# Moving the split of the gated output and the order of scores and values in a two-layer hybrid encoder step

## The chip, the cores and the metric

The kernel runs on one core of a Trainium2 chip. The metric is the device time of one execution in microseconds. Engines are named as the profile names them: PE (TensorE, with PEld for its weight loads), ACT (ScalarE), DVE (VectorE), POOL (GpSimd) and SP (SyncE). SP issues nearly all loads of weights; POOL issues the loads of the caches, the small stores and the DMAs that finish a transposition.

## What is computed

The reference is one inference step of a two-layer trunk over 384 rows: 256 rows of a new stream ("prompt") and 8 x 16 rows of running streams ("sample"), each of width 2048, all in float32.

```python
# layer 0
p = rmsnorm(h) @ w_in0          # q, k, v, gate of 8 forgetting heads, the same of 8 stick-breaking heads, 8 forget logits
fo = softmax(q k^T * scale + F_q - F_k, causal) v              # per head; sample rows also see 128 cached rows
so = exp(log_sigmoid(z) + sum of log_sigmoid(-z) after it) v   # z = q k^T * scale, strictly causal
h = h + concat(fo * silu(fz), so * silu(sz)) @ w_out0
# layer 1
u, v, z = split(rmsnorm(h) @ w_in1)
h = h + (u * (W_s layernorm(v) + b) * silu(z)) @ w_out1
y = rmsnorm(h)
```

The keys, the values and the log forget gates of layer 0 and the normalised v of the sample rows are outputs too.

## The kernel before

**Products.** The 384 rows are three blocks of 128 (`NT`). A product with a weight matrix runs over columns in blocks of 512 and over the depth in units of 128 rows. Each float32 operand is split into a high part in a reduced float32 format (`F32R`) and the rest: ACT copies the high part (L84 for weights), DVE subtracts (L86). Each unit then takes three matmuls per row block (L101 to L103): high by high, high by rest, rest by high. `dense_nat` runs one column block: for each pair of units it calls `wunit` twice (load on SP, split) and `products` once. It accumulates into three PSUM banks of the pool "d", which has four. Its argument `between` maps a depth index to a function that is called ahead of that pair; the instructions traced in it are ordered, each on its own engine, behind the last weight split that was traced. Weight buffers: five "raw", four "whi", four "wlo".

**Layer 0.** It runs in four groups of four heads (`quad`), groups 0 and 1 forgetting heads, 2 and 3 stick-breaking heads. A group projects k and q (`turned`), v (`values`), runs its four heads (`head`) and projects the gate. A projection is evicted from PSUM by ACT (`evict`, L400). k and q are then turned (`turn`): one DVE block transposition into a slot and 16 DMAs issued on POOL (L127). The gate becomes silu on ACT and DVE (L459 to L464), is multiplied with the heads' outputs `mixn` (L465), and is turned into `mT`, which shares its one buffer with the turned q. `mT` is split into a high and a rest part (`mixhi`, `mixlo`; L473, L474) for the output product `w_out0`. Behind that come the projections of the next group.

**A head.** POOL builds the forget mask `fb` (L486 to L492); DVE transposes the cached keys (L499); PE computes scores of prompt and sample rows into two banks of the pool "a", which has four (L503 to L508). DVE and ACT make probabilities `pr` (L520 to L526, or L530 to L541). PE transposes them (L545), ACT copies them to `PT` (L547), PE multiplies with the values (L553 to L561), DVE puts the result into `mixn` (L564 to L567). The cached keys and values (`kcache`, `vcache`) and `fb` have two buffers each.

**Output product of layer 0.** Its first two column blocks are done in two parts: the depth units 0 to 11 for both (`early`), then 12 to 15 (`rest`). The second block accumulates in three banks of the pool "a".

**Order.** The program is traced in the order of the code; a planner with costs of its own then sets the order of instructions on each engine, by that order as priority and by what it takes to be ready. Only `tc.issue_after` (used by `then` at the start and by `between`) fixes an order by hand. Engines run their queues in order.

**Start.** x is loaded in pieces on SP and, for the sample rows of the first two pieces, on ACT's queue (L154). The load of the norm's gains `graw` is the first on ACT's queue (L163). PE transposes the gains (L167) and x (L211); ACT and DVE make the high part and the rest (L214, L215); the first product is that of k of group 0, columns 1024 to 1535.

## Time and profile before

| | before |
|---|---|
| median of 3 runs | 1888.44 us (1886.86 to 1889.18) |
| profiled execution | 1889.66 us |
| its span | 1887.9 us |
| PE busy | 1816.4 us, 96% of the span |
| DVE busy | 922.8 us, 49% |
| ACT busy | 726.2 us, 38% |
| POOL busy | 401.2 us, 21% |
| mean granted clock of PE | 0.981 |
| layer 0's heads, first scores to last values | 150.5 to 705.0 us |

The profile is that of one execution. A row of a group or of the timeline names the source line, the engine, the operation, the tile that is written and the tiles that are read, and the shape; "xN" is the number of instructions in it. In brackets stands the time that the engine was idle before, and what released it. A releaser is inferred from the semaphore events: where an instruction waits for several, it is the one that came last. A matmul of plain float32 operands shows as two records, one of reduced operands as one; records of a stream overlap, so the pace is read from their starts.

### The profile page before, as it was taken

To read this page: it belongs to the slowest core of one execution; us is meant where nothing else is said; L and a number is where in the kernel's file an instruction comes from. 1 tells how busy PE (TensorE), PEld (TensorE's weight loads), DVE (VectorE), ACT (ScalarE), POOL (GpSimd) and SP (SyncE) were. 2 spreads that over 40 slices of the span, in tenths; PEclk is the share of its full clock that TensorE was granted. 3 is DMA by queue.
4 is the path that set the end of the run, shared out by engine and by line. 5 is a ranking of instruction groups with operands and counts; after the bars stand their busy time and mean duration, and the time that the engine had idled before them with its cause. 6 is when DMAs were issued, how large, how long until landed. Compare 5 with 4: busy or idle time off the path is not lost. (4 is left out here: it accounts for less than half of the span.)

```text
span 1887.9 us, 24617 instructions
## 1 busy us (share of the span) xinstructions
PE 1816.4 (96%) x8655; PEld 1497.2 (79%) x8655; DVE 922.8 (49%) x1541; ACT 726.2 (38%) x1294; POOL 401.2 (21%) x640
## 2 busy tenths in 40 slices
PE   8999599989959989999999999999999999999998
PEld 6987487878848868888888888888888888888887
DVE  4445434634643564553443535535644563554466
ACT  4435233534623544443333333232333333333334
POOL 1543633332152102220020013202102210220020
PEclk9999799999979989999999999999999999999999
DMA  5866556655545537764444345445535544454543
GB/s 177 212 172 160 140 163 176 171 146 165 148 123 156 151 90 226 206 189 128 129 138 125 123 141 155 140 137 146 153 124 153 143 140 150 139 141 134 178 143 120
DMA packets 160140, 285.63 MB, mean 151 GB/s; under 512 B 23768, under 2 KB 39056, under 8 KB 160016
## 3 DMA queue, kind: packets, MB, share of 16 engines
q1 hardware_dynamic: 127424, 225.37, 40.2%
q0 software_dynamic: 25072, 54.10, 11.3%
q10 hardware_dynamic: 7520, 4.60, 0.8%
q8 instruction: 68, 1.11, 0.3%
q14 instruction: 56, 0.46, 0.1%
HBM read 253.50 MB, written 14.74 MB: 142 GB/s over the span
## 5 line engine op out<-in xcount | busy, mean ns | idle before, releaser
L102 PE MATMUL d<-wlo,slot 128*128 128x512 f32 x2352 | 923.7, 394 | 0.1
L103 PE MATMUL d<-whi,slot 128*128 128x512 f32 x2352 | 916.7, 391 | 0.0
L86 DVE TENSOR_TENSOR wlo<-raw,whi 128x512 fp32r<-128x512 f32 x784 | 540.5, 698 | 769.0 <-ACT whi L84 768.3
L101 PE MATMUL d<-whi,slot 128*128 128x512 f32 x2352 | 826.1, 393 | 43.0 <-ACT slot L400 41.8
L84 ACT ACTIVATE whi<-raw 128x512 fp32r<-128x512 f32 x784 | 494.2, 631 | 909.0 <-PE d L103 843.4
L101 PEld LDWEIGHTS d<-whi,slot 128*128 128x128 f32 x2352 | 443.8, 189 | 138.9 <-ACT slot L400 42.7
L102 PEld LDWEIGHTS d<-wlo,slot 128*128 128x128 f32 x2352 | 444.2, 189 | 94.0 <-issue 1.2
L103 PEld LDWEIGHTS d<-whi,slot 128*128 128x128 f32 x2352 | 443.9, 189 | 94.1 <-issue 2.5
L127 POOL DMA_DIRECT2D gTt<-trn x128 | 78.2, 618 | 446.4 <-issue 262.8
L127 POOL DMA_DIRECT2D qT<-slot x64 | 39.1, 619 | 83.1 <-DVE slot L124 81.7
L127 POOL DMA_DIRECT2D mT<-slot x64 | 39.1, 618 | 49.8 <-issue 40.3
L127 POOL DMA_DIRECT2D kT<-slot x64 | 39.3, 621 | 8.1 <-DVE slot L124 3.2
L706 POOL DMA_DIRECT2D wr<-in_w_sp_dram x64 | 35.0, 554 | 27.7 <-DVE wT L710 25.9
L699 DVE TENSOR_TENSOR slot<-d,slot 128x512 f32<-128x512 f32 x48 | 32.0, 687 | 12.4 <-PE d L103 12.4
L656 POOL DMA_DIRECT2D slot<-in_sgu_ln_g_dram x8 | 4.5, 566 | 134.0 <-PE d L103 134.0
L428 POOL DMA_DIRECT2D vcache<-in_cache_sb_v_dram x8 | 7.2, 896 | 120.5 <-PE a L557 102.2
L426 POOL DMA_DIRECT2D kcache<-in_cache_sb_k_dram x32 | 25.1, 791 | 18.9 <-DVE KT L499 12.3
L545 PE MATMUL a<-ident,pr 128*128 128x128 f32 x96 | 17.8, 284 | 11.5 <-ACT pr L541 10.0
L380 PE MATMUL d<-wlo,slot 128*128 128x264 f32 (+1 forms) x96 | 27.2, 286 | 0.6 <-DVE wlo L91 0.6
L379 PE MATMUL d<-whi,slot 128*128 128x264 f32 (+1 forms) x96 | 26.7, 287 | 0.5 <-ACT slot L400 0.5
L381 PE MATMUL d<-whi,slot 128*128 128x264 f32 (+1 forms) x96 | 26.8, 283 | 0.0
L545 PEld LDWEIGHTS a<-ident,pr 128*128 128x128 f32 x96 | 12.7, 144 | 17.2 <-ACT pr L541 11.3
(228 smaller groups left out, 1202.1 us busy)
## 6 DMA issues: line engine op xcount, KB each, us to landing
raw<-in_w_in_dram SPq DMA_DIRECT2D x640, 256.0 KB, 2.8
raw<-in_w_out_dram SPq DMA_DIRECT2D x189, 256.0 KB, 3.4
gTt<-trn POOLq DMA_DIRECT2D x128, 48.0 KB, 3.5
kcache<-in_cache_fox_k_dram POOLq DMA_DIRECT2D x32, 128.0 KB, 5.5
vcache<-in_cache_fox_v_dram POOLq DMA_DIRECT2D x8, 512.0 KB, 4.5
kcache<-in_cache_sb_k_dram POOLq DMA_DIRECT2D x32, 128.0 KB, 4.8
vcache<-in_cache_sb_v_dram POOLq DMA_DIRECT2D x8, 512.0 KB, 4.7
kT<-slot POOLq DMA_DIRECT2D x64, 48.0 KB, 4.2
```

Source lines behind the costliest of these rows:

```text
L84: highs.append(S.activation(hi, raw, AF.Copy).ins)
L86: splits.append(V.tensor_tensor(out=lo, in0=raw, in1=f32(hi), op=ALU.subtract).ins)
L101: PE.matmul(o, lhsT=his[k][:, t], rhs=hi[:, 0, :], start=(k == first), stop=False)
L102: PE.matmul(o, lhsT=his[k][:, t], rhs=lo[:, 0, :], start=False, stop=False)
L103: mm = PE.matmul(o, lhsT=los[k][:, t], rhs=hi[:, 0, :], start=False, stop=(k == last))
L127: G.dma_start(dst[32 * j:32 * j + 32, :, 32 * a:32 * a + 32], trn[32 * a:32 * a + 32, :, 32 * j:32 * j + 32])
L379: PE.matmul(o, lhsT=h, rhs=hi[:, kk, :n], start=(k == 0), stop=False)
L380: PE.matmul(o, lhsT=h, rhs=lo[:, kk, :n], start=False, stop=False)
L381: PE.matmul(o, lhsT=l, rhs=hi[:, kk, :n], start=False, stop=(k == KT - 1))
L545: PE.transpose(b[:, o:o + P], pr[:, j * P:(j + 1) * P], ident)
L699: evicted = V.tensor_tensor(out=h1[c][:, tb, :], in0=o[tb], in1=h1[c][:, tb, :], op=ALU.add)
L706: G.dma_start(wr[js, 0, :].rearrange("p (a s) -> p a s", s=32), w_sp[g, :, js].rearrange("(a p) s -> p a s", p=32))
```

## The change

Three things are changed, all in layer 0.

1. The split of the gated output leaves the end of its group and becomes a function `mix_split`. It is called in the next group's q projection ahead of depth index 8, and for the last group in the second column block of the early output product ahead of depth index 6. `mixhi` and `mixlo` are replaced by two lists that `mix_split` fills.
2. `head` becomes a generator that stops once the probabilities of its head are made. The loop over heads first starts head hh (its cache loads, mask, scores and probabilities) and then lets head hh - 1 go on (transposes, values). The tile `pr` has four buffers in place of two.
3. At the start, seven products of a tile of ones with itself (128 x 128, plain float32) are put first on PE, and five more between the transposes of the first two depth units of x and the first product. The load of the gains goes behind the first piece of x.

```diff
-        nc.scalar.dma_start(graw[:, 0, :], norm0_g.rearrange("(k p) -> k p", p=P))
...
+        def keep_warm(n):
+
+            b = bank()
+            for _ in range(n):
+                then("PE", lambda: PE.matmul(b[:, :P], lhsT=ones, rhs=ones, start=True, stop=True))
+
+        keep_warm(7)
         load_piece(0)
+        nc.scalar.dma_start(graw[:, 0, :], norm0_g.rearrange("(k p) -> k p", p=P))
...
         done = [x_transposes(k) for k in range(2)]
+        keep_warm(5)
...
-            qT, _ = turned(base, rstdq, "qT")
+            qT, _ = turned(base, rstdq, "qT", between={8: mix_split} if g else None)
...
-            for hh in range(4):
-                hs = slice(hh * P, hh * P + P)
-                head(g, h0 + hh, kT[:, hh], vnat[:, :, hs], qT[:, hh], *cached(hh), mixn[:, :, hs])
+            heads = []
+            for hh in range(5):
+
+                if hh < 4:
+                    hs = slice(hh * P, hh * P + P)
+                    heads.append(head(g, h0 + hh, kT[:, hh], vnat[:, :, hs], qT[:, hh], *cached(hh), mixn[:, :, hs]))
+                    next(heads[hh])
+                if hh:
+                    next(heads[hh - 1], None)
...
-            mixhi.append(slot().rearrange("p (k t) -> p k t", k=4))
-            mixlo.append(slot().rearrange("p (k t) -> p k t", k=4))
-            mT = t.rearrange("p (t k) q -> p k t q", k=4)
+            mixed.append(t.rearrange("p (t k) q -> p k t q", k=4))
+
+        mixed = []
+
+        def mix_split():
+            mT = mixed.pop(0)
+            hi, lo = slot().rearrange("p (k t) -> p k t", k=4), slot().rearrange("p (k t) -> p k t", k=4)
             for k in range(4):
-                h3 = mixhi[g][:, k, :].rearrange("p (t q) -> p t q", q=P)
+                h3 = hi[:, k, :].rearrange("p (t q) -> p t q", q=P)
                 S.activation(h3, mT[:, k], AF.Copy)
-                V.tensor_tensor(out=mixlo[g][:, k, :].rearrange("p (t q) -> p t q", q=P), in0=mT[:, k], in1=f32(h3), op=ALU.subtract)
+                V.tensor_tensor(out=lo[:, k, :].rearrange("p (t q) -> p t q", q=P), in0=mT[:, k], in1=f32(h3), op=ALU.subtract)
+                mh.append(hi[:, k, :])
+                ml.append(lo[:, k, :])
...
-                    pr = tmp("pr")
+                    pr = tmp("pr", 4)
...
+                prs.append(pr)
+            yield
+            for dec in (0, 1):
+                pr = prs[dec]
                 b = bank()
...
-                dense_nat(w_out0, 0, c * 512, mh, ml, out=outs[c], ks=ks)
+                dense_nat(w_out0, 0, c * 512, mh, ml, nk=KT, out=outs[c], ks=ks, between={6: mix_split} if c and ks is early else None)
```

More of the change, by code (lines that the diff above doesn't have):

```diff
@@ L356, in forget @@
                 G.dma_start(nFcd[:, hs, :], nFc)
-        mixhi, mixlo = [], []
+        mh, ml = [], []
         def hk(x, k):
@@ L393, in quad, with project @@
             ko_p, vo_p, ko_s, vo_s = (fk_p, fv_p, fk_s, fv_s) if fox else (sk_p, sv_p, sk_s, sv_s)
-            def project(c0):
-                return first if c0 == 1024 else dense_nat(w_in0, 0, c0, h0h, h0l)
+            def project(c0, between=None):
+                return first if c0 == 1024 else dense_nat(w_in0, 0, c0, h0h, h0l, between=between)
             def evict(o, dst, scale, n=512):
@@ L404, in store, with turned @@
                 G.dma_start(o_s[:, :, h0:h0 + 4, :].rearrange("b q h d -> (b q) (h d)"), nat[:, 2, :])
-            def turned(c0, scale, tag, outs=None):
+            def turned(c0, scale, tag, outs=None, between=None):
                 nat = slot(F32).rearrange("p (t c) -> p t c", t=NT)
-                evict(project(c0), nat, scale)
+                evict(project(c0, between), nat, scale)
                 if outs:
@@ L509, in head @@
                           start=True, stop=True)
-            PTs = []
+            PTs, prs = [], []
             rs = {}
@@ L539, in head @@
                     V.tensor_tensor(out=z, in0=z, in1=l, op=ALU.add)
-                    pr = tmp("pr")
+                    pr = tmp("pr", 4)
                     S.activation(pr, z, AF.Exp)
+                prs.append(pr)
+            yield
+            for dec in (0, 1):
+                pr = prs[dec]
                 b = bank()
@@ L570, in tile_hybrid_step @@
             quad(g)
-        mh = [mixhi[k // 4][:, k % 4, :] for k in range(KT)]
-        ml = [mixlo[k // 4][:, k % 4, :] for k in range(KT)]
         h1 = [slot(F32).rearrange("p (t c) -> p t c", t=NT) for _ in range(4)]
@@ L630, in tile_hybrid_step @@
             load_x(h1[c], c * 512, 512)
-            residual(c, dense_nat(w_out0, 0, c * 512, mh, ml, between={6: lambda: h1_transposed(0), 14: lambda: h1_transposed(1)} if c == 2 else {14: lambda: h1_transposed(2)}))
+            residual(c, dense_nat(w_out0, 0, c * 512, mh, ml, KT, between={6: lambda: h1_transposed(0), 14: lambda: h1_transposed(1)} if c == 2 else {14: lambda: h1_transposed(2)}))
         calc_rstd(ssq1)
```

## The prediction

> **What bounds the kernel now.** I read the engines' shares first, then what TensorE (PE) waited for, then the order of time around its longest waits, then the granted clock in the stretches behind them.

> ```profile
> PE 1816.4 (96%) x8655; PEld 1497.2 (79%) x8655; DVE 922.8 (49%) x1541; ACT 726.2 (38%) x1294; POOL 401.2 (21%) x640
> ```

> PE is busy in 1816.4 of 1887.9 us, so 71.5 us of idle time, and whatever ran at a lowered clock, are all that a reordering can win. The waits of PE:

> ```profile
> PE d L101 <- ACT slot L400: 41.8, 3, 18.0
> PE a L545 <- ACT pr L541: 10.0, 3, 4.3
> PE a L167 <- POOL mp L259: 3.9, 1, 3.9
> PE a L553 <- ACT PT L547: 1.7, 3, 0.6
> PE a L545 <- ACT pr L524: 1.4, 2, 1.0
> PE a L211 <- DMA slot<-in_x_sample_dram: 1.4, 1, 1.4
> ```

> The columns are total us, times, longest. Three waits of 41.8 us in all are put down to L400, the eviction of a projection out of PSUM by ScalarE (ACT). Three evictions take 1.82 us (below), so ACT was held up before them. The end of the first group of heads, in order of time:

> ```profile
> 205.01 0.40 PE L103 MATMUL d<-whi,slot 128*128 128x512 f32 x1
> ...
> 209.92 0.63 PE L560 MATMUL a<-vnat,PT 128*128 128x128 f32 x2
> 210.35 0.63 PE L561 MATMUL a<-vnat,PT 128*128 128x128 f32 x2
> ...
> 215.44 9.76 POOL L127 DMA_DIRECT2D mT<-slot  x16 [0.93 <-DVE slot L124]
> 226.61 1.76 ACT L473 ACTIVATE slot<-mT 128x384 fp32r<-128x384 f32 x4 [18.13 <-DMA mT<-slot]
> ...
> 228.28 1.82 ACT L400 ACTIVATE slot<-d,rstd 128x512 f32<-128x512 f32 x3
> 229.00 0.80 PE L101 MATMUL d<-whi,slot 128*128 128x512 f32 x1 [18.02 <-ACT slot L400]
> ```

> The next group's k projection was complete at 205.4. Its eviction stands in ACT's queue behind the split of the gated output (L473), which waits for 16 turning DMAs (9.76 us to issue on POOL) that start only when the last head has ended at 210.98. From that end to the split it is 15.6 us, and PE, with three of four "d" banks waiting to be evicted, stands still. The second and third group end likewise:

> ```profile
> 364.80 0.39 PE L561 MATMUL a<-vnat,PT 128*128 128x128 f32 x2
> 377.76 0.39 PE L103 MATMUL d<-whi,slot 128*128 128x512 f32 x1
> 381.91 1.76 ACT L473 ACTIVATE slot<-mT 128x384 fp32r<-128x384 f32 x4 [5.81 <-DMA mT<-slot]
> ...
> 531.98 0.40 PE L103 MATMUL d<-whi,slot 128*128 128x512 f32 x1
> 536.85 0.39 PE L561 MATMUL a<-vnat,PT 128*128 128x128 f32 x2
> 552.51 1.76 ACT L473 ACTIVATE slot<-mT 128x384 fp32r<-128x384 f32 x4 [17.06 <-DMA mT<-slot]
> ```

> The second group's heads ended 13 us before the projection did, so there the wait is only 6.15 us. The fourth group ends in layer 0's output product, where nothing is to be evicted in that way; there the last head's own chain is bare:

> ```profile
> 695.83 0.90 PE L545 MATMUL a<-ident,pr 128*128 128x128 f32 x3 [4.30 <-ACT pr L541]
> 700.45 0.90 PE L545 MATMUL a<-ident,pr 128*128 128x128 f32 x3 [3.73 <-ACT pr L541]
> ```

> After each of these PE runs at half clock for a while. Windows, with PE's busy time, PE's weight loads, DVE, ACT, POOL, and then the granted clock:

> ```profile
> 8.65:14.70 6.05, 6.05 (x17) 4.65 (x18) 2.78 (x6) 2.54 (x5) 0.00 (x0) 1.00 0.99 345
> 209.26:210.98 1.72, 1.72 (x14) 1.36 (x6) 1.04 (x2) 0.00 (x0) 1.72 (x3) 0.50 0.63 169
> 229.00:233.16 4.16, 4.16 (x10) 3.29 (x11) 1.91 (x2) 1.10 (x2) 2.27 (x4) 0.50 0.46 189
> 384.30:390.17 5.87, 5.87 (x14) 4.61 (x15) 1.90 (x2) 1.10 (x2) 3.98 (x7) 0.50 0.43 158
> 554.89:560.84 5.95, 5.95 (x14) 4.69 (x15) 1.91 (x2) 1.11 (x2) 4.05 (x7) 0.50 0.43 156
> 693.96:707.61 13.65, 7.48 (x43) 5.65 (x44) 6.76 (x12) 3.38 (x7) 0.00 (x0) 0.50 0.00 1
> 100.00:150.00 50.00, 50.00 (x222) 41.42 (x221) 21.13 (x26) 16.95 (x27) 18.60 (x28) 1.00 0.60 163
> ```

> In full flow PE does 222 matmuls in 50 us, 0.225 us each; the half-clock rows show 10 in 4.16 us, 0.42 us each. The first row says clock 1.00, but its 17 matmuls in 6.05 us are 0.36 us each: PE was cold there too, before the clock's first record.

> **The change part by part.** The profiled execution took 1889.66 us (span 1887.9 and 1.8 around it); the median of the runs is 1888.44, 1.2 lower. The sum goes from 1889.66.

> *The split moved.* The 4 ACT and 4 DVE instructions of the split are kept; they now stand behind the weight splits of the first 8 units of the next group's q projection (in the last group, of the first 6 of the output product's second block). The eviction of k no longer has them ahead of it, so the three waits go: 41.8. What is late next is the split itself: ACT comes to it, waits for the turned data, and the weight splits from unit 8 on are queued behind it, DVE's halves too. PE's cover is 8 units, 72 matmuls, 72 x 0.225 = 16.2 us, in the last group 54, 12.2 us. The next high halves take 0.63 us each:

> ```profile
> L84 ACT ACTIVATE whi<-raw 128x512 fp32r<-128x512 f32 x784 | 494.2, 631 | 909.0 <-PE d L103 843.4
> ```

> Had the heads ended as late as now, with the covering products straight behind them, the data would come 15.6 us after the last head; with 1.8 us for the split on ACT and 1.3 for two high halves, PE would be short by 15.6 + 1.8 + 1.3 - 16.2 = 2.5 us in the first group, 2.2 in the third (552.51 - 537.24 = 15.3), nothing in the second, and 6.5 in the last: 11 us. If the heads end some 7 us earlier against the products, it is nothing. I take 3, between 0 and 11: the earlier end is what the next part brings, but not surely by that much everywhere.

> *The half clock behind the waits.* 4.16 + 5.87 + 5.95 = 15.98 us at half rate, done in half the time: 8.0 back. These stretches exist only because of the waits; bounds 0 (if equal idle time appears elsewhere) and 8.0.

> *Scores ahead of values.* No instruction is added; two more "pr" buffers. One head of the first group:

> ```profile
> 150.53 0.59 PE L503 MATMUL a<-kT,qT 128*128 128x256 f32 x2
> 157.43 0.38 PE L545 MATMUL a<-ident,pr 128*128 128x128 f32 x2
> 166.66 0.42 PE L553 MATMUL a<-vnat,PT 128*32 128x128 f32 x8
> 168.23 0.60 PE L503 MATMUL a<-kT,qT 128*128 128x256 f32 x2
> ```

> Head 0 takes 16 us from scores to values, and head 1's scores come only then. With them in front of head 0's transposes, the two chains overlap; a head then costs roughly the 7 to 9 us that lie between scores and transposes or between transposes and values, instead of 18. The matmuls that fill the gaps stay the same in number, so while there are fillers PE gains nothing; the gain is at each group's end, where the fillers are used up. The bare waits of the tails are 10.0 + 1.7 + 1.4 = 13.1 us; I take 9 back, between 0 (heads no faster against the fillers) and 13.1. Their half clock: 1.72 us in the first group and 7.48 busy us in the fourth, half of it 4.6; I take 3.5, between 0 and 4.6. An earlier end of the heads is also what brings the split's data in time.

> *Ones at the start.*

> ```profile
> 3.92 0.25 PE L167 MATMUL a<-ident,graw 16*128 16x16 f32 x1 [3.92 <-POOL mp L259]
> 6.35 1.11 PE L211 MATMUL a<-ident,slot 128*128 128x128 f32 x4 [1.37 <-DMA slot<-in_x_sample_dram]
> 8.65 0.80 PE L101 MATMUL d<-whi,slot 128*128 128x512 f32 x1 [1.19 <-ACT whi L219]
> ```

> A full f32 product of 128 columns is two records; cold it takes 210.35 - 209.92 = 0.43 us. Seven take 3.0 us, inside the 3.9 us before the first transpose. Five take 2.1 us cold or about half of that warm, against the 1.2 us ahead of 8.65: up to 0.9 us late if still cold. The gains' load goes behind one x_sample load on ACT's queue; it is needed together with those columns and stays in their shadow. If PE is warm from the first product, 6.05 / 2 = 3.0 us come back. The DMA engines' share there is 0.99, so faster products may wait for weights. I take 1.5, between -0.9 and 3.0.

> [...]

> **Sum.** 41.8 + 8.0 + 9 + 3.5 + 1.5 - 3 = 60.8; less 1 for a small new wait at a place that I can't name, 59.8: 1889.66 - 59.8 = 1829.9, about 1830. With all terms at their best the gain is 41.8 + 8.0 + 13.1 + 4.6 + 3.0 = 70.5, 1819; with the small terms at their worst (0, 0, -0.9, -11) it is 38, 1852.

> **Rivals.**

> *A. The heads end no earlier against the fillers,* since the program's order puts scores wherever it sees PE free. The tails stay, and the split's place costs 11: 41.8 + 8.0 + 1.5 - 11 = 40.3, 1849. For it: the order of all engines is the planner's, which put L473 before L400 where that cost 18 us. Against it: in the second group the heads already ended 13 us before the fillers.

> *B. The turning DMAs of k go before those of the gated output on POOL.* k is now evicted before or about when the heads end, so both sets of 16 stand ready together. 9.76 us more before the split at four places, less some slack where the heads end early: 4 x 9.76 = 39 at most, and the half clock after each, 8.0 / 3 = 2.7 us a place, 50 in all. With three quarters of it, 1830 + 38 = 1868. Against it: the output's turn is earlier in the program's order.

> *C. The wait stays under another name:* the eviction of k is planned behind another instruction of ACT that needs the last head. 41.8 and 8.0 are not won, the tails and the start are, and the 1 us lost: 1889.66 - (9 + 3.5 + 1.5 - 1) = 1877.

> *D. Slower: scores ahead block PE.* Scores need the cache's keys transposed:

> ```profile
> L426 POOL DMA_DIRECT2D kcache<-in_cache_fox_k_dram x32: 786/790/872, 54.5 to 301.9; - x32
> L499 DVE STREAM_TRANSPOSE KT<-kcache x32: 670/700/712, 97.6 to 671.5; 128x512 f32<-128x512 f32 x32
> ...
> DMA to landing us min/median/max: 2.8/5.2/7.8
> ```

> (ns of one, min, median and max; then us from issue to landing.) PE takes its queue in order: if scores of head h+1 stand before the values of head h and the keys come late, values, fillers and the release of the vcache buffer are all held. Four issues, landing and two transposes are 3.2 + 5.2 + 1.4 = about 10 us, and the new pace would be 7 to 9. Twelve heads have one ahead of them; it decides against the change from 60 / 12 = 5 us lost at each. At 6 us: 1830 + 72 = 1902. Against it: kcache has two buffers, so keys can be fetched a head ahead, and no such wait is among PE's now.

> **How the numbers follow.** Forecast 0.68 (1819 to 1840), A 0.14, B 0.06, C 0.04, D 0.08. A difference under 0.2% (3.8 us) can't be told from no change here. Faster is the forecast, A, B and most of C, 0.90; mixtures of D and the forecast give 0.03 for no change; slower 0.07. The range is 1818 to 1865: the best sum, and up to a case between A and B; it leaves out the rest of B, C and D.

> **What would show it.** The PE waits for L400 at the ends of groups one to three are gone (or, by C, return with another instruction before them). L473 starts behind the weight splits of unit 7, with a wait for the turned data under 2 us (A: several; B: over 9, with the turn of k just before). The next scores start before the values of the head ahead, and less than 12 us lies between two heads' scores (A: 15 or more). Half clock is seen only at the start and the end. PE's first products come 0.225 us apart before 12 us. If PE's idle time is above 35 us, the forecast is wrong, and D shows as waits of PE before L503 or L508.

## The result and the profile after

The changed kernel takes 1821.9 us (median of 4 runs, 1821.1 to 1823.4) against 1888.8 us before: a ratio of 0.9648, with a 95% interval of 0.9631 to 0.9665. The profiled execution took 1821.09 us with a span of 1819.4, 68.5 us shorter than the span before. The forecast was 1830; the time lies inside the range, 8 us below the forecast and 3 us above the best sum.

The first lines of the page of the changed kernel, and below them PE's granted clock in 40 equal slices, in tenths:

```profile
span 1819.4 us, 24664 instructions
...
PE 1807.4 (99%) x8679; PEld 1490.8 (82%) x8679; DVE 922.0 (51%) x1541; ACT 723.1 (40%) x1294; POOL 400.9 (22%) x640
...
PEclk9999999999999999999999999999999999999999
```

PE's idle time fell by 59.5 us, from 71.5 to 12.0: 54.9 of that are the three waits (41.8) and the tails of the heads (13.1). Its busy time fell by 9.0 us although the ones added 24 records of 3.36 + 1.28 = 4.6 us; the 13.6 us less for all else are mostly the half clock, for which the prediction had 8.0 and at most 4.6. The longest of what PE still waits for, again with total us, times and longest:

```profile
PE a L195 <- DVE ones L133: 1.1, 1, 1.1
PE d L386 <- ACT slot L407: 0.8, 1, 0.8
PE a L336 <- DVE logf L331: 0.3, 1, 0.3
PE a L165 <- POOL md L266: 0.3, 1, 0.3
```

Every wait of layer 0's heads and at the ends of its groups is gone; the rows for L407 and `logf` belong to the forget logits ahead of the first heads. The line numbers have moved: L407 is the eviction (L400 before), L490 the split (L473), L522 the scores, L568 the transposes, L576 to L584 the values. The end of the first group of heads, in order of time (ACT's and POOL's rows):

```profile
199.90 0.69 ACT L407 ACTIVATE slot<-d,rstd 128x512 f32<-128x512 f32 x1 [0.74 <-PE d L103]
202.62 0.69 ACT L407 ACTIVATE slot<-d,rstd 128x512 f32<-128x512 f32 x1
202.99 9.74 POOL L127 DMA_DIRECT2D mT<-slot  x16
...
214.28 1.85 POOL L127 DMA_DIRECT2D kT<-slot  x3
217.08 7.91 POOL L127 DMA_DIRECT2D kT<-slot  x13 [0.95 <-DMA mT<-slot]
...
223.56 1.75 ACT L490 ACTIVATE slot<-mT 128x384 fp32r<-128x384 f32 x4
```

k is evicted as soon as its product is done; the gated output's 16 DMAs go ahead of k's; the split comes when ACT reaches its place, and no wait stands beside it: POOL's last wait for one of those DMAs had ended at 217.08, 6 us earlier.

The same work lies between two marks further on. The first and last evictions of layer 1's v, before and after:

```profile
L646 ACT ACTIVATE vt<-d,rstd x24: 690/690/692, 843.1 to 1073.6; 128x512 f32<-128x512 f32 x24
```

```profile
L667 ACT ACTIVATE vt<-d,rstd x24: 671/690/692, 775.1 to 1004.6; 128x512 f32<-128x512 f32 x24
```

By 775 us the gain is 68.0 us; at the end of the span it is 68.5. All of it arises in layer 0, and nothing takes it back later.

### The profile page after: what moved, and what is told of

Read it like the earlier page. It is cut to its first block, busy times and chain, and to the rows that moved or that the text cites. A ratio compares the mean times of both kernels' runs of the same rounds, so it can differ in the third digit from the quotient of the medians.

```text
span 1819.4 us, 24664 instructions
## 1 busy us (share of the span) xinstructions
PE 1807.4 (99%) x8679; PEld 1490.8 (82%) x8679; DVE 922.0 (51%) x1541; ACT 723.1 (40%) x1294; POOL 400.9 (22%) x640
## 3 DMA queue, kind: packets, MB, share of 16 engines
q8 instruction: 68, 1.11, 0.3%
## 5 line engine op out<-in xcount | busy, mean ns | idle before, releaser
L103 PE MATMUL d<-whi,slot 128*128 128x512 f32 x2352 | 914.7, 390 | 0.0
L84 ACT ACTIVATE whi<-raw 128x512 fp32r<-128x512 f32 x784 | 494.1, 631 | 919.0 <-PE d L103 861.9
L101 PE MATMUL d<-whi,slot 128*128 128x512 f32 x2352 | 820.4, 390 | 0.1
L101 PEld LDWEIGHTS d<-whi,slot 128*128 128x128 f32 x2352 | 441.6, 188 | 92.8 <-issue 1.2
L103 PEld LDWEIGHTS d<-whi,slot 128*128 128x128 f32 x2352 | 441.7, 188 | 92.5 <-issue 2.1
L127 POOL DMA_DIRECT2D gTt<-trn x128 | 78.0, 617 | 446.5 <-issue 264.5
L127 POOL DMA_DIRECT2D qT<-slot x64 | 39.0, 617 | 70.2 <-DVE slot L124 48.8
L127 POOL DMA_DIRECT2D mT<-slot x64 | 39.0, 617 | 47.2 <-PE d L103 29.8
L127 POOL DMA_DIRECT2D kT<-slot x64 | 39.1, 618 | 12.8 <-DMA kT<-slot 4.5
L608 POOL DMA_DIRECT2D blk<-h1d x12 | 10.9, 918 | 70.3 <-DMA h1d<-slot 34.1
L433 POOL DMA_DIRECT2D kcache<-in_cache_fox_k_dram x32 | 25.3, 795 | 4.4 <-DVE KT L518 3.2
```

The costliest lines, as they stand in the source:

```text
L84: highs.append(S.activation(hi, raw, AF.Copy).ins)
L101: PE.matmul(o, lhsT=his[k][:, t], rhs=hi[:, 0, :], start=(k == first), stop=False)
L103: mm = PE.matmul(o, lhsT=los[k][:, t], rhs=hi[:, 0, :], start=False, stop=(k == last))
L127: G.dma_start(dst[32 * j:32 * j + 32, :, 32 * a:32 * a + 32], trn[32 * a:32 * a + 32, :, 32 * j:32 * j + 32])
L433: G.dma_start(k[32 * j:32 * j + 32].rearrange("p (b d) -> p b d", d=32), kc[:, :, h0 + hh, 32 * j:32 * j + 32].rearrange("b (i p) d -> p ( ...
```

## The experiments

### The split alone

In the kernel before, the split becomes `mix_split` and goes to its new places; heads and start stay as they were.

```diff
-            qT, _ = turned(base, rstdq, "qT")
+            qT, _ = turned(base, rstdq, "qT", between={8: mix_split} if g else None)
...
-                dense_nat(w_out0, 0, c * 512, mh, ml, out=outs[c], ks=ks)
+                dense_nat(w_out0, 0, c * 512, mh, ml, nk=KT, out=outs[c], ks=ks, between={6: mix_split} if c and ks is early else None)
```

> The kernel before with the split alone moved to its fixed place; heads and start as before. Theory (the split ahead of k's eviction made the three waits; the heads' tails are a matter of the order of scores and values): the 41.8 us of waits for L400 and the 8.0 us of half clock go, the tails of 13.1 us stay, and the split at its place costs 0 to 11 us, because the heads end as late as before. 1889 - 49.8 + (0 to 11) = 1839 to 1850. Rival (the split's place is all that matters, the tails come with it): 1825, the changed kernel without its start.

Measured: 1841.6 us, ratio 0.9749 (0.9734 to 0.9764), 47.4 us less than the 1889.05 beside it. PE's waits, and where the split stands on ACT:

```profile
PE a L551 <- ACT pr L547: 10.0, 3, 4.3
...
PE a L559 <- ACT PT L553: 2.5, 4, 0.8
PE a L551 <- ACT pr L530: 1.4, 2, 1.0
```

```profile
233.12 1.31 ACT L84 ACTIVATE whi<-raw 128x512 fp32r<-128x512 f32 x2 [2.77 <-PE d L103]
234.34 1.75 ACT L477 ACTIVATE slot<-mT 128x384 fp32r<-128x384 f32 x4
```

The wait for L400 is gone, and the heads' tails are all there, 13.9 us of them. The split costs nothing: in the first group it starts at 234.3 us, 23.2 us after the heads' last product ended (211.1), behind the last of q's 16 weight splits. The fixed place is behind the eighth, so the planner put the split later than it was forced to. In front of it ACT had waited for PE, not for the data: this was in time though the heads ended as late as before. The half clock does not go as a whole. Windows with PE's busy time first after the length, and the granted clock third from the end:

```profile
209.36:212.77 3.41, 3.41 (x19) 2.92 (x12) 2.65 (x6) 0.97 (x2) 3.40 (x5) 0.50 0.64 172
...
506.32:513.15 6.83, 6.25 (x41) 4.80 (x39) 3.71 (x6) 2.22 (x4) 1.60 (x2) 0.50 0.30 68
...
649.68:659.92 10.24, 5.31 (x38) 3.97 (x39) 3.45 (x7) 3.37 (x7) 0.00 (x0) 0.50 0.11 43
```

The tails alone still let the clock fall at the ends of groups one, three and four: 14.97 us of PE's work at half clock, against 1.72 + 7.48 in the tails before, which costs half of the difference, 2.9 us. The wait for `PT` grew by 0.8. That gives 41.8 + 8.0 - 2.9 - 0.8 = 46.1, and the spans of the two profiled executions (1887.9 and 1842.1) are 45.8 us apart. The profiled execution is the slowest of the four.

### Scores ahead of values alone

The other half: the generator, the loop over five steps and the four `pr` buffers; the split stays at its group's end.

```diff
...
-                head(g, h0 + hh, kT[:, hh], vnat[:, :, hs], qT[:, hh], *cached(hh), mixn[:, :, hs])
...
+                if hh < 4:
+                    hs = slice(hh * P, hh * P + P)
+                    heads.append(head(g, h0 + hh, kT[:, hh], vnat[:, :, hs], qT[:, hh], *cached(hh), mixn[:, :, hs]))
+                    next(heads[hh])
+                if hh:
+                    next(heads[hh - 1], None)
...
```

> The kernel before with scores ahead of values alone; the split stays at the end of its group, ahead of k's eviction. Theory: the tails go (13.1 us of waits, 4.6 of half clock). The heads end earlier against the products, so in the second and third group the turned data is there before k's projection ends, and those waits go too (6.2 + 17.7); in the first group the heads end only about 23 matmuls before the projection does, and 10 to 13 us of 18 stay. 1889 - 17.7 - 23.9 - (5 to 8) - 5.9 = about 1835. Rival 1 (the heads' order is enough, the split's place is not needed): 1825. Rival 2 (the eviction waits for the split in every group as long as the split is traced ahead of it, whatever the heads do): over 1860.

Measured: 1838.35 us, ratio 0.9732 (0.9718 to 0.9747), 50.7 us less. The waits of PE, and the one that is left, in order of time:

```profile
PE d L101 <- ACT slot L400: 11.3, 3, 10.8
```

```profile
204.64 9.72 POOL L127 DMA_DIRECT2D mT<-slot  x16 [4.20 <-DVE slot L124]
...
215.88 1.76 ACT L479 ACTIVATE slot<-mT 128x384 fp32r<-128x384 f32 x4 [10.51 <-DMA mT<-slot]
...
217.54 1.82 ACT L400 ACTIVATE slot<-d,rstd 128x512 f32<-128x512 f32 x3
218.26 0.29 PEld L101 LDWEIGHTS d<-whi,slot 128*128 128x128 f32 x1 [11.27 <-ACT slot L400]
218.26 0.80 PE L101 MATMUL d<-whi,slot 128*128 128x512 f32 x1 [10.85 <-ACT slot L400]
```

As the theory had it, one of the three waits is left, 10.8 us in the first group. In the second and third group the data is there when ACT comes to the split, and PE waits 0.23 us; here the second:

```profile
366.56 1.75 ACT L479 ACTIVATE slot<-mT 128x384 fp32r<-128x384 f32 x4
368.22 1.81 ACT L400 ACTIVATE slot<-d,rstd 128x512 f32<-128x512 f32 x3
368.94 0.50 PE L101 MATMUL d<-whi,slot 128*128 128x512 f32 x1 [0.23 <-ACT slot L400]
```

The eviction still stands right behind the split, so both rivals fall: the heads' order alone is not enough, and the wait does not stay in every group. No wait on `pr` or `PT` is left in PE's list, so the tails are wholly a matter of the order of scores and values.

### Split and heads together

The changed kernel with the start of the kernel before.

```diff
-        keep_warm(7)
         load_piece(0)
-        nc.scalar.dma_start(graw[:, 0, :], norm0_g.rearrange("(k p) -> k p", p=P))
...
         done = [x_transposes(k) for k in range(2)]
-        keep_warm(5)
```

> The changed kernel without the ones and with the gains' load first. Theory: the start is a term of its own, so 1821.9 + 3.2 = 1825. If the gains of split (39 to 50) and heads (about 54) were separate, 1889 - 95 would come out; they share the three waits, so their sum is capped at the idle time and half clock of the before, about 64 without the start.

Measured: 1824.2 us, ratio 0.9654 (0.9638 to 0.967), 64.9 us less. The single gains are 47.4 and 50.7, in sum 98.1: 33 us are in both. They are the shared waits: of 41.8 us each part alone removes all or 41.8 - 11.3 = 30.5, and the half clock behind the second and third is in both as well, (5.87 + 5.95) / 2 = 5.9; that makes 36, near the 33. From the split alone to both together it is 17.5 us, against 13.1 + 4.6 = 17.7 for the tails and their half clock.

### The start alone

The ones and the moved load of the gains in the kernel before.

```diff
-        nc.scalar.dma_start(graw[:, 0, :], norm0_g.rearrange("(k p) -> k p", p=P))
...
+        keep_warm(7)
         load_piece(0)
+        nc.scalar.dma_start(graw[:, 0, :], norm0_g.rearrange("(k p) -> k p", p=P))
...
         done = [x_transposes(k) for k in range(2)]
+        keep_warm(5)
```

> The kernel before with the ones and the moved load of the gains alone. Theory: the clock is up from the first product on, and the first projection is evicted 3.2 us earlier, as in the changed kernel (50.07 against 53.30 us); nothing after it takes that back: 1885.5. Rival (the waits further on absorb it, or the ones fill no window): 1888 to 1889.

Measured: 1887.8 us, ratio 0.9995 (0.9986 to 1.0005): no difference that the runs resolve, and not the 3.2 us expected. The profile shows why. PE's first instructions in this kernel:

```profile
1.11 3.36 PE L195 MATMUL a<-ones 128*128 128x128 f32 x14 [1.11 <-DVE ones L133]
5.08 0.26 PE L165 MATMUL a<-ident,graw 16*128 16x16 f32 x1 [0.62 <-POOL md L266]
5.27 1.54 PE L217 MATMUL a<-ident,slot 128*128 128x128 f32 x6
6.60 2.34 PE L195 MATMUL a<-ones 128*128 128x128 f32 x10
8.60 0.78 PE L101 MATMUL d<-whi,slot 128*128 128x512 f32 x1
9.17 0.63 PE L102 MATMUL d<-wlo,slot 128*128 128x512 f32 x1
```

The five products took 2.34 us, so PE was still cold, and the first product (8.60) started no earlier than before (8.65). In the changed kernel the same ten records took 1.28 us and the first product came at 7.54. The trace's clock records put the rise to full speed at 10.2 us here and at 6.0 us there. Both lie on the grid of 3.41 us that the last section shows, and a window is one step of it: here PE was busy for 2.80 us in the window from 3.40 to 6.82 us and the clock stayed down, there for 3.08 us in the window from 2.59 to 6.00 and it rose. All profiles of this study together (us from the span's start):

```
ones   kernel                   clock rises   first eviction
yes    changed kernel               6.0          50.07
yes    start alone                 10.2          51.55
yes    no fixed place               4.6          49.95
yes    nine ones                    6.5          50.70
no     before                      14.7          53.30
no     split alone                 14.8          53.13
no     heads alone                 12.0          51.71
no     split and heads             13.7          52.67
no     ones in the waits           13.2          52.16
```

The mean of the first eviction is 50.6 with ones and 52.6 without: 2.0 us for the start, with a spread of 1.6 us in either group that goes with the time at which the clock rises. The waits of the groups absorb next to nothing of it: the lead of this run over the kernel before is 1.75 us at the first eviction, 1.07 at the fourth (120.64 against 121.72), and still 0.99 at the last one of layer 0's groups (656.66 against 657.64). The start is thus worth 1.3 (this run) to 2.3 us (changed kernel against split and heads, 1821.9 and 1824.2), and neither of the two differences is resolved by the runs.

### Ones inside the waits

Does the half clock behind a wait cost anything of its own? In the first and third group of the kernel before, PE is given something to do while it waits, and q's products are ordered behind that.

```diff
+        def ones_after(ins, n):
+            b = bank()
+            for _ in range(n):
+                with tc.issue_after(ins):
+                    ins = PE.matmul(b[:, :P], lhsT=ones, rhs=ones, start=True, stop=True).ins
+            return ins
...
+                if c0 == base and fill[0] is not None:
+                    with tc.issue_after(fill[0]):
+                        return dense_nat(w_in0, 0, c0, h0h, h0l)
...
-                head(g, h0 + hh, kT[:, hh], vnat[:, :, hs], qT[:, hh], *cached(hh), mixn[:, :, hs])
+                values_end[0] = head(g, h0 + hh, kT[:, hh], vnat[:, :, hs], qT[:, hh], *cached(hh), mixn[:, :, hs])
+            fill[0] = ones_after(values_end[0].ins, 64) if g in (0, 2) else None
```

> The kernel before, and behind the last value product of the first and the third group 64 products of ones (plain float32, 128 x 128), ordered ahead of the next group's q products: they run inside the two waits of 18 us and leave the waits themselves alone. Theory (half clock behind a wait is a cost of its own): the two half-clock stretches of 4.16 and 5.95 us shrink to little, and half of them, 5 us, comes back: 1884; 3 to 6 us if the ones do not fill the waits exactly. Rival (the half clock does not set the time there, something else does): 1889.

Measured: 1884.9 us, ratio 0.9978 (0.9968 to 0.9988), 4.1 us less. The first group, as PE runs it:

```profile
209.45 15.27 PE L393 MATMUL a<-ones 128*128 128x128 f32 x128
224.48 0.48 PE L101 MATMUL d<-whi,slot 128*128 128x512 f32 x1
224.79 0.39 PE L102 MATMUL d<-wlo,slot 128*128 128x512 f32 x1
...
227.97 0.50 PE L101 MATMUL d<-whi,slot 128*128 128x512 f32 x1 [0.49 <-ACT slot L412]
228.30 0.40 PE L102 MATMUL d<-wlo,slot 128*128 128x512 f32 x1
228.54 0.39 PE L103 MATMUL d<-whi,slot 128*128 128x512 f32 x1
228.77 0.40 PE L101 MATMUL d<-whi,slot 128*128 128x512 f32 x1
```

The product that waits for the eviction starts at 228.0 us (229.0 before), no further ahead than this execution already was at its first eviction (52.16 against 53.30). But the products behind it start 0.23 us apart in place of 0.43. So the half clock is a cost of its own: 4.1 us measured, 5 expected, the rival's 0 outside the interval. The 4.1 is not its exact price: q's first products no longer fill the third group's tail, and PE waits 4.32 us for `pr` there in place of 2.00.

### No fixed place, and nine ones

Two variants of the changed kernel. In the first the split is traced in the same place but not ordered by hand; in the second nine products stand first in place of seven.

```diff
-                with tc.issue_after(splits[-1]), tc.issue_after(highs[-1]):
-                    behind = between[kp]() or ()
+                if between[kp] is mix_split_of[0]:
+                    between[kp]()
+                else:
+                    with tc.issue_after(splits[-1]), tc.issue_after(highs[-1]):
+                        behind = between[kp]() or ()
```

> The changed kernel, where the split is traced at the same places of the next group but not ordered by hand behind the weight splits of the unit ahead; the planner may put it earlier. Theory (what matters is that k's eviction is traced ahead of the split, and the turned data is there in time because the heads end early): the same time, 1822, no wait for L400 or for the split. Rival (the fixed place is what keeps ACT from being blocked): the waits come back in part, 3 to 12 us more.

Measured: 1822.05 us, ratio 0.9643 (0.9627 to 0.9659): the changed kernel's time. In the first group the split starts at the same moment:

```profile
223.58 1.75 ACT L494 ACTIVATE slot<-mT 128x384 fp32r<-128x384 f32 x4
```

The fixed place, behind the eighth weight split of q, does not bind: that one ended on ACT at 211.4 us in the changed kernel, and in both kernels the planner put the split at 223.6. It is enough to trace the split in q's projection, behind k's eviction; no run traced it between the two.

```diff
-        keep_warm(7)
+        keep_warm(9)
```

> The changed kernel with nine ones ahead of the gains' transposition in place of seven, so that the gap of 0.3 to 0.6 us in front of that transposition is filled. Theory (the clock rises at the end of a window of 3.41 us that PE has nearly filled, and its phase against the start differs between executions): the rise comes at the first or second window's end, before 8 us in the profile; the time is 1820.5 to 1822, at most 1 us better. Rival (the two more products delay the gains and the first x transposes): 0.5 to 1 us slower.

Measured: 1822.1 us, ratio 0.9644 (0.963 to 0.9658), the same again. The gap ahead of the gains is filled and the rise comes at 6.5 us, behind a window (3.04 to 6.45) in which PE was busy for all 3.41 us, but the first product moves from 7.54 to 8.04, and the first eviction is inside the spread of the table above. Neither theory's difference can be told at this size.

## Why the prediction was right, and where its sizes were off

*What bounds the kernel* was read rightly: the three waits, the half clock behind them and the heads' tails were nearly all that could be won, and nearly all was. The gain by the spans is 68.5 us; the sum had 59.8. Against these 8.7 us more, three terms of the sum come to 9.2: 3 for the split, 5.2 for the tails and 1 for a place that was not named.

*When k was complete.* The prediction took 205.4 us for the end of k's projection. This reading is off, though no term of the sum hangs on it. The last twelve products ahead of that mark are q's, for which one bank of "d" was free: where q's products are ordered behind the ones, twelve of them run there, from 224.48 us on, before the next one waits for the eviction. In the kernel before, k's last product (L103) started at 198.96 us, and the eviction that ran at 228.28 had been ready for about 29 us.

*The split moved: 41.8.* Shown by the split alone, where the waits for L400 are gone, and by the heads alone, where the one that stays has the split right in front of the eviction.

*The split late at its new place: 3 taken, 0 measured.* This is the step that was worked out wrongly. It took the place behind unit 7 as the place where ACT meets the split. It is only the earliest: with the split alone, heads as late as before, the split came 23.2 us after the heads had ended, when the data was there. In the changed kernel it came behind the fourteenth weight split of q. The 11 us bound was never near. What saved these 3 us with the split alone was thus not the earlier end of the heads, as the prediction reasoned, but the planner's choice, which it did not foresee: that part is luck.

*The half clock: 8.0.* The ones inside two of the waits gave 4.1 back of their 5. In the split alone part of it came back at the tails, so it belongs to waits and tails together rather than to the waits alone; the changed kernel has none until the end of the span.

*Scores ahead of values: 9 and 3.5 taken, 13.1 and 4.6 there.* Mis-sized. Nothing of a tail is left in the changed kernel, and 17.5 us were measured from the split alone to both. The pace that the prediction gave (7 to 9 us a head, under 12) was too short: scores and values of the first group in the changed kernel are

```profile
166.03 0.60 PE L522 MATMUL a<-kT,qT 128*128 128x256 f32 x2
176.23 0.43 PE L576 MATMUL a<-vnat,PT 128*32 128x128 f32 x8
177.80 0.38 PE L522 MATMUL a<-kT,qT 128*128 128x256 f32 x1
188.25 0.43 PE L576 MATMUL a<-vnat,PT 128*32 128x128 f32 x8
195.61 0.43 PE L576 MATMUL a<-vnat,PT 128*32 128x128 f32 x8
```

about 12 us apart, against 15 to 19 before. That was enough: the last values end at 197.3, ahead of k's last product, and the end of the chain is covered. Each head's scores stand before the values of the head ahead of it; the first two heads of this group have their scores done together.

*The start: 1.5 taken, 2.0 by the mean of the profiles,* with a spread of 1.6 us between executions. The start alone gave the least: its first eviction (51.55) came 0.2 us ahead of the earliest one without ones (51.71). The five kernels without ones start alike, and their clocks rise between 12.0 and 14.8 us.

*The 1 us for a place that could not be named:* there was none.

*Rivals.* A (heads no earlier against the fillers) is refuted by the tails' end. B (k's turn ahead of the output's on POOL): the first group's rows show the output's 16 DMAs at 202.99 and k's from 214.28. C: no wait for an eviction is left in the groups. D: in the changed kernel PE waits neither for keys nor ahead of scores.

What stays open is why the planner, where the split is traced ahead of k's eviction, keeps it ahead although the eviction is ready earlier. The runs show that the order of the trace decides, not what in the planner makes it so.

## What to carry to other kernels

Where an engine that evicts PSUM stands still in front of a transfer, ask whether the waiting instruction is needed soon; if its result is needed a stage later, trace it a stage later, behind the evictions. Price such a stall with its half clock (here 15.98 us of it behind 41.8 us of waits), and look at two cures for one stall together: here each alone gave about 50 us and both gave 65. In a chain of equal items (scores, probabilities, values), put the first step of the next item ahead of the last step of this one; while other work fills the gaps it gains nothing, and at the end, when that is used up, it gains the whole tail (13.1 us of waits here).

## What the runs showed of the hardware

```profile
205.85:209.26 3.41, 1.61 (x28) 1.05 (x28) 1.03 (x5) 2.07 (x6) 3.40 (x6) 1.00 0.58 56
7.88:11.29 3.41, 2.64 (x6) 1.83 (x7) 2.03 (x4) 1.24 (x3) 0.00 (x0) 1.00 1.06 365
376.52:379.93 3.41, 1.62 (x8) 1.01 (x6) 0.30 (x1) 0.00 (x0) 3.20 (x6) 1.00 0.81 221
533.53:536.94 3.41, 1.98 (x32) 1.55 (x33) 0.71 (x3) 1.01 (x2) 0.24 (x1) 1.00 0.13 49
```

```profile
502.90:506.32 3.42, 1.42 (x8) 0.88 (x6) 2.15 (x4) 1.22 (x3) 0.00 (x0) 1.00 0.69 181
```

PE was busy for 1.61 and 1.42 us in the windows behind which the clock fell, for 1.62 and 1.98 us in those behind which it stayed up. In the eight traces other than that of split and heads together, it was busy for at most 1.63 us in the 23 windows behind which the clock fell (1.63 in the start alone, 204.79 to 208.21 us), and for at least 1.62 us in the 4,218 behind which it stayed up. Upward, 2.64 us did not raise it, and 3.08 us raised it in the changed kernel (2.59 to 6.00 us) but 3.09 did not in the split alone (7.97 to 11.38): PE's busy time as the profile models it does not tell these two apart:

```profile
2.59:6.00 3.41, 3.08 (x15) 2.77 (x15) 0.68 (x3) 0.08 (x1) 2.75 (x11) 1.00 1.01 322
```

```profile
7.97:11.38 3.41, 3.09 (x7) 2.06 (x8) 1.60 (x3) 0.78 (x2) 0.00 (x0) 1.00 1.09 372
```
